# A two-layer hybrid decoder trunk: seven block products in place of eight for most chunk pairs, the residual stream in DRAM, tables and factors by ACT's DMA queue

## The chip, the cores and the metric

The kernel runs on one core of one Trainium2 chip. The metric is the device time of one execution in microseconds (us), median of three runs. TensorE (PE) has one of two clock levels granted to it, 1.2 and 2.4 GHz; the profile gives the granted share of full speed. The other engines are VectorE (DVE), ScalarE (ACT), GpSimd (POOL) and SyncE (SP), which issues DMAs.

## The reference, cut to what matters

256 tokens of width 2048 go through two layers. Each layer has a mixer sub-layer and an FFN sub-layer, all in f32.

```python
for l in range(2):
    h = rms_norm(x, g_mix_pre)                       # (256, 2048)
    proj = h @ w_in                                  # 2048 -> 512 pool | 1024 conv GLU | 4x1024 q k v gate | 3x2048 branch gates
    y_pool = pool_mixer(u_pool) @ w_pool_proj        # 512 -> 2048, window tables
    y_conv = conv_module(u_conv) @ w_conv_proj       # GLU, 31 causal taps, LayerNorm, swish; 512 -> 2048
    y_ret = retention(q, k, v, g_ret) @ w_ret_proj   # 8 heads, decay tables; 1024 -> 2048
    merged = sigmoid(gate0)*y_pool + sigmoid(gate1)*y_conv + sigmoid(gate2)*y_ret
    x = x + rms_norm(merged @ w_out, g_mix_post)     # 2048 -> 2048
    h = rms_norm(x, g_ffn_pre)
    a, b = split(h @ w_ffn_in)                       # 2048 -> 2 x 5632
    x = x + rms_norm((silu(a) * b) @ w_ffn_out, g_ffn_post)   # 5632 -> 2048
```

## The kernel before

**Products.** Tokens lie in two halves h = 0 and 1 of 128. A weight matrix is worked off in chunks of 512 columns; a chunk has one step for each 128 rows k of the weight. At a step each half multiplies its transposed activations (128x128, stationary) by the weight block (128x512, moving). Both are split into a rounded part `hi` and the rest `lo` in f32r, and one step of one half is three matmuls in `product`: hi by hi (L747), lo by hi (L748), hi by lo (L749). `multiply(h)` does one step of one half; half 1 runs `LAG` = 8 steps behind half 0. A step of both halves is called an item here.

**Weights.** `fetch` brings two steps of weights (512 KB) into one of 6 `raw` tiles by SP's DMA queue (L692); `load` makes `whi` on ACT (L725) and `wlo` on DVE (L726) for both steps, which is called a block here. There are 7 buffers of each, and `load_ahead` keeps 7 blocks ahead of half 1.

**Seven products (Strassen-Winograd).** For a pair of neighbouring chunks, two token halves, and one quad of four k, there are 2x2 times 2x2 blocks, which is eight block products of two steps each. `mixed_product` does seven (`b11`, `b21`, `t1`, `b22`, `t2`, `t3`, `t4`), each of two steps of three matmuls. It costs sums of weight blocks on DVE (L705, L712, L729, L730), three further casts to hi and lo, sums of results (L785, L790, L792, L797 on DVE, one ACT copy L770 into a `dt` tile), and one addition more per result (L578, L588). The sums of token blocks (`token_sums`, tile pair `S`) are made once for each input. Before the change this is done for k 12 to 15 of 10 of the 11 FFN-in pairs of each layer (the set `fast`); the first pair after a sub-layer's start is `paired` instead, that is, its two chunks take turns step by step.

**Order.** `chunks` lists the whole program. A layer is: pool, v, q, k, retention gate, conv gate and conv value chunks; then for each branch and column chunk a gate chunk and a projection (4 or 8 steps); 4 chunks of `w_out`; then FFN in four parts of 3, 3, 3 and 2 pairs of FFN-in, each followed by 4 FFN-out chunks over that part's hidden quads, accumulated in `og` tiles.

**Side work.** `pool_job`, `conv_job`, `ret_job` are generators; after each item of half 1 `run_jobs` gives them `BUDGET` = 0.35 of credit, in list order, at most two heavy ones at a time; a `WAIT` pauses a job for 8 ticks (a tick is one `multiply`). The conv job is 124 yields of 0.35 for its taps (L342) and 4.0 for its rest; the retention jobs of a layer cost 10.4 together. `finish` runs a job to its end at once when a chunk needs it. Transposes and splits of results are put off by `defer` (7 ticks for the hidden quads, 14 for merged quads and rotated q and k).

**Tiles.** A pool of 20 `slot` tiles of 4 KB per partition holds transposed activations (8 per input), branch results, q, k, v, hidden quads, `og`. Tag `dt` has two buffers: window and decay tables, and the two result sums of a mixed pair. The gain rows `gp` have two buffers. The residual `x0`, `x1` stays in SBUF. All DMAs go by SP's queue: weights L692, tables L378, L402, L415, pool weights L372, gain rows L548.

Of the kernel before, what the change touches and what calls it, by code (L numbers as in the profile page):

```python
# [18 lines left out]
P = 128  # L19
# [18 lines left out]
LAG = 8  # L38
WBLOCKS = 7
SLOTS = 20  # L40
# [10 lines left out]
N_WARM = 12  # L51

# [23 lines left out]
def trunk(ctx: ExitStack, tc: tile.TileContext, x, x_cols, positions, g_mix_post, g_ffn_post, w_in, pool_w,  # L76
# [38 lines left out]
    xs = []  # L115
    for h in range(2):
        xs.append(cpool.tile([P, 4, NB], F32, name=f"x{h}"))
# [25 lines left out]
    def square_sum(src, acc):  # L143
        j = t2("junk", 1)
        act.activation(j, src, ACT.Square, accum_out=acc)
# [14 lines left out]

    def pre_norm_quad(h, c, gain, mixed):
        tp, g = transpose4(xs[h][:, c, :]), gain[:, 4 * c:4 * c + 4]
        if not (mixed and c == 3):
            st["xT", h].append(split(tp, g))
            return
        if h == 0:
            st["u"] = slot([P, 2, 4, P])
        u = st["u"][:, h]
        dve.tensor_tensor(u, tp, g.unsqueeze(2).to_broadcast([P, 4, P]), op=ALU.mult)
        st["xT", h].append(split(u))  # L170
        if h == 1:
            defer(6, token_sums)

    def token_sums():

        u = st["u"]
# [3 lines left out]
        dve.tensor_tensor(s[:, 1], s[:, 0], a11, op=ALU.subtract)  # L180
        dve.tensor_tensor(s[:, 2], a11, a21, op=ALU.subtract)
        dve.tensor_tensor(s[:, 3], a12, s[:, 1], op=ALU.subtract)
        hi, lo = slot([P, 4, 2, P], F32R), slot([P, 4, 2, P], F32R)
        act.copy(hi, s)
        dve.tensor_tensor(lo, s, hi.bitcast(F32), op=ALU.subtract)
        st["S"] = (hi, lo)
# [6 lines left out]
    def sum_squares(h):  # L193
        ssq = small("ssq_n", 4)
        for c in range(4):
            square_sum(xs[h][:, c, :], ssq[:, c:c + 1])
        pre_norm_rstd(h, ssq)

    def load_x(h, c):
        nc.sync.dma_start(xs[h][:, c, :], x[0, h * P:(h + 1) * P, c * NB:(c + 1) * NB])  # L200
# [19 lines left out]
    def post_norm(h, gain, mixed=False):  # L220
# [3 lines left out]
        def residual(c):  # L224
            xc = xs[h][:, c, :]
# [14 lines left out]
        defer(N_FIRST + N_STEP * 4, sum_squares, h)  # L240

# [153 lines left out]
    def ret_job(l, h, qd):  # L395
# [4 lines left out]
        if h == 0:  # L400
            dt = t2("dt", 2, (P, 4, P))
            nc.sync.dma_start(dt, decays[qd])  # L402
# [110 lines left out]
    def ev_swish(l, qd):  # L513
        def f(h, ps):
# [5 lines left out]
            add_job(("ret", h), ret_job(l, h, qd))  # L520
        return f

    def ev_gate(h, ps):
        s = t2("sg", 3)
# [437 lines left out]
```

## Time and profile before

| | |
|---|---|
| median of 3 runs | 2876.71 us (2876.64 to 2877.05) |
| the profiled execution, its own time | 2875.82 us |
| its span, first to last instruction | 2874.1 us |
| mean granted TensorE clock | 0.999 |
| PE busy | 2855.9 us (99%) |
| DVE busy | 1947.7 us (68%) |
| ACT busy | 1356.4 us (47%) |
| DMA | 555.07 MB, 193 GB/s |

Busy time is the union of an engine's instructions. Matmuls overlap one another in the records, so their spacing is read from start to start. PEld is TensorE's weight load. SPq is SP's DMA issue queue.

### The profile page before, as it was taken

How to read it: one execution, taken by the hardware profiler on the slowest of the kernel's cores; microseconds unless marked ns; L12 is line 12 of the kernel's file. 1: busy time of each engine (PE TensorE's matmuls, PEld its weight loads, DVE VectorE, ACT ScalarE, POOL GpSimd, SP SyncE). 2: the span in 40 equal slices, each digit the busy share in tenths (PEclk: the TensorE clock that was granted, in tenths of full speed). 3: DMA queues.
4: the chain of work that ended last, by engine and by line, in shares of the span. 5: the costliest groups of instructions: out<-in, count | busy, mean ns of one | idle time of the engine just before them, and what ended most of it. 6: DMA issues, size and time to landing. Idle time of an engine off the chain costs nothing.

```text
span 2874.1 us, 34293 instructions
## 1 busy us (share of the span) xinstructions
PE 2855.9 (99%) x12932; PEld 2362.9 (82%) x12932; DVE 1947.7 (68%) x2253; ACT 1356.4 (47%) x1547; POOL 83.1 (3%) x102
## 2 busy tenths in 40 slices
PE   9999999999999999999999999999999999999998
PEld 7788888888888888888888888888888888888887
DVE  6766965555775776857765569555567757668586
ACT  5444445444644544544554444444455454445353
POOL 0000000000000000000000000001000000000000
PEclk9999999999999999999999999999999999999999
DMA  8655565556565656555655555655565555666554
GB/s 298 193 183 176 186 199 189 191 189 203 174 204 174 215 196 201 176 203 175 229 188 185 189 171 188 199 189 186 191 204 190 190 185 189 211 194 200 187 183 153
DMA packets 289862, 555.07 MB, mean 193 GB/s; under 512 B 17824, under 2 KB 21152, under 8 KB 289696
## 3 DMA queue, kind: packets, MB, share of 16 engines
q1 hardware_dynamic: 289696, 552.89, 58.5%
q8 instruction: 101, 1.65, 0.2%
q14 instruction: 65, 0.53, 0.1%
HBM read 550.72 MB, written 2.10 MB: 192 GB/s over the span
## 4 chain that ended last, share of the span: by engine, by line
PE 98%; DVE 1%; DMA 0%; POOL 0%; ACT 0%; issue 0%; SPq 0%; DVEq 0%; POOLq 0%; ACTq 0%
PE mm L748 32%; PE mm L749 32%; PE mm L747 32%; PE tp L140 2%; DVE x L226 0%; PE sc L429 0%; PE tp L421 0%; PE sc L385 0%; DVE wlo L726 0%; DVE ta L131 0%; DMA dt<-in_bands 0%; DMA par<-in_params 0%; POOL rpost_a L210 0%; PE sc L411 0%; PE tp L406 0%
## 5 line engine op out<-in xcount | busy, mean ns | idle before, releaser
L726 DVE TENSOR_TENSOR wlo<-raw,whi 128x1024 fp32r<-128x1024 f32 (+1 forms) x1085 | 1336.9, 1240 | 738.0 <-ACT whi L725 725.6
L725 ACT CAST whi<-raw 128x1024 fp32r<-128x1024 f32 (+1 forms) x1085 | 1135.4, 1052 | 1283.5 <-PE mm L748 1148.2
L747 PE MATMUL mm<-whi,slot 128*128 128x512 f32 x4056 | 1589.9, 392 | 1.9 <-ACT whi L725 1.7
L748 PE MATMUL mm<-whi,slot 128*128 128x512 f32 x4056 | 1581.1, 390 | 0.2
L749 PE MATMUL mm<-wlo,slot 128*128 128x512 f32 x4056 | 1580.9, 390 | 0.0
L749 PEld LDWEIGHTS mm<-wlo,slot 128*128 128x128 f32 x4056 | 761.8, 188 | 159.4 <-DVE wlo L726 0.7
L747 PEld LDWEIGHTS mm<-whi,slot 128*128 128x128 f32 x4056 | 762.0, 188 | 156.7 <-ACT whi L725 2.4
L748 PEld LDWEIGHTS mm<-whi,slot 128*128 128x128 f32 x4056 | 762.4, 188 | 156.1 <-DVE slot L134 2.1
L342 DVE SCALAR_TENSOR_TENSOR slot<-slot,par,slot 128x229 f32<-128x229 f32 (+23 forms) x240 | 101.9, 479 | 0.3
L134 DVE TENSOR_TENSOR slot<-tp,slot 128x512 fp32r<-128x512 f32 x60 | 41.2, 687 | 50.3 <-ACT slot L133 50.3
L133 ACT CAST slot<-tp 128x512 fp32r<-128x512 f32 x60 | 35.2, 586 | 83.3 <-PE tp L140 83.3
L538 POOL TENSOR_TENSOR slot<-slot,tb 128x512 f32<-128x512 f32 x32 | 43.3, 1352 | 639.5 <-DVE tb L537 639.5
L578 DVE TENSOR_TENSOR ta<-dt,mm 128x512 f32<-128x512 f32 x40 | 27.4, 684 | 29.9 <-PE mm L749 29.9
L218 POOL TENSOR_SCALAR ms_o<-ssq_t 128x1 f32<-128x1 f32 x8 | 3.2, 395 | 1509.0 <-DVE ssq_t L216 1509.0
L525 ACT ACTIVATE sg<-mm,rstd 128x512 f32<-128x512 f32 x48 | 33.0, 688 | 24.4 <-PE mm L749 24.2
L597 DVE TENSOR_TENSOR slot<-slot,mm 128x512 f32<-128x512 f32 x48 | 32.8, 684 | 13.0 <-PE mm L749 13.0
L140 PEld LDWEIGHTS tp<-ident,ta 128*128 128x128 f32 x272 | 34.0, 141 | 8.4
L140 PE MATMUL tp<-ident,ta 128*128 128x128 f32 x272 | 40.6, 271 | 0.0
L569 ACT ACTIVATE sg<-ta,rstd 128x512 f32<-128x512 f32 x40 | 29.0, 725 | 10.5 <-DVE ta L588 10.5
L580 DVE SCALAR_TENSOR_TENSOR ta<-ta,rstd,sg 128x512 f32<-128x512 f32 x40 | 30.0, 749 | 1.0
L133 ACT CAST slot<-ta 128x512 fp32r<-128x512 f32 x36 | 22.4, 621 | 16.4 <-DVE ta L131 16.2
L537 DVE TENSOR_TENSOR tb<-mm,sg 128x512 f32<-128x512 f32 x32 | 22.1, 690 | 9.4 <-PE mm L749 8.1
(131 smaller groups left out, 732.5 us busy)
## 6 DMA issues: line engine op xcount, KB each, us to landing
raw<-in_w_in SPq DMA_DIRECT2D x367, 512.0 KB, 3.5
raw<-in_w_ffn_in SPq DMA_DIRECT2D x352, 512.0 KB, 4.4
raw<-in_w_ffn_out SPq DMA_DIRECT2D x176, 512.0 KB, 3.7
raw<-in_w_out SPq DMA_DIRECT2D x64, 512.0 KB, 3.6
raw<-in_w_ret_proj SPq DMA_DIRECT2D x32, 512.0 KB, 3.6
raw<-in_w_pool_proj SPq DMA_DIRECT2D x16, 512.0 KB, 3.6
raw<-in_w_conv_proj SPq DMA_DIRECT2D x16, 512.0 KB, 3.8
dt<-in_decays SPq DMA_DIRECT2D x12, 256.0 KB, 3.8
```

Of the source, the lines that this page charges most:

```text
L133: act.copy(t[:, 0], src)
L134: dve.tensor_tensor(t[:, 1], src, t[:, 0].bitcast(F32), op=ALU.subtract)
L140: pe.transpose(tp[:, j, :], src[:, j * P:(j + 1) * P], ident)
L342: dve.scalar_tensor_tensor(acc[:, ct, s:], hT[:, ct, :SEQ - s], w[:, TAPS - 1 - s:TAPS - s], acc[:, ct, s:], op0=ALU.mult, op1=ALU.add)
L525: act.activation(s, ps, ACT.Sigmoid, scale=st["rstd", h])
L538: gp.tensor_tensor(m, m, t, op=ALU.add)
L597: dve.tensor_tensor(o, o, ps, op=ALU.add)
L725: act.copy(hi[:, kk:kk + step], raw[:, kk:kk + step])
L726: dve.tensor_tensor(lo[:, kk:kk + step], raw[:, kk:kk + step], hi[:, kk:kk + step].bitcast(F32), op=ALU.subtract)
L747: pe.matmul(ps, a[0], w[0], start=first, stop=False)
L748: pe.matmul(ps, a[1], w[0], start=False, stop=False)
L749: pe.matmul(ps, a[0], w[1], start=False, stop=stop)
```

## The change

Seven products in place of eight are used for more pairs: in each layer 5 pairs of gate chunks (the chunk order is changed so that gates 0 and 1 of a column chunk stand together, and gates 2 in twos), chunks 0 and 1 of `w_out`, 10 FFN-in pairs as before, and 5 pairs of FFN-out, where FFN now has three parts of 4, 4 and 3 pairs. For `w_out` and FFN-out the mixed quad is the first, k 0 to 3. `token_sums` becomes a light job and is run for six inputs a layer. The conv chunks come right after the pool chunk. The residual no longer stays in SBUF: it is stored to DRAM by SP's queue after each sub-layer but the last (`store_x`) and fetched by ACT's queue into slot tiles near the end of the next (`fetch_x`). There are 24 slots. Window and decay tables, pool weights and gain rows are loaded by ACT's queue.

```diff
-SLOTS = 20
+SLOTS = 24
...
-    xs = []
-    for h in range(2):
-        xs.append(cpool.tile([P, 4, NB], F32, name=f"x{h}"))
+    dram = ctx.enter_context(tc.tile_pool(name="stream", bufs=1, space=bass.MemoryType.DRAM))
+    xd = [[x[0, h * P:(h + 1) * P, :] for h in range(2)]]
+    for n in range(2 * DEPTH - 1):
+        xd.append([dram.tile([P, D], F32, name=f"x{n}_{h}") for h in range(2)])
...
+    def fetch_x(n, h):
+
+        st["x", h] = []
+        for c2 in range(2):
+            t = slot([P, 2, NB])
+            nc.scalar.dma_start(t, xd[n][h][:, columns(c2)].rearrange("p (c n) -> p c n", n=NB))
+            st["x", h].append(t)
+
+    def store_x(n, h, tiles):
+        for c2 in range(2):
+            nc.sync.dma_start(xd[n][h][:, columns(c2)].rearrange("p (c n) -> p c n", n=NB), tiles[c2])
...
+        st["xT", h].append(split(transpose4(x_block(h, c)), gain[:, 4 * c:4 * c + 4]))
+        if mixed and c == 3 and h == 1:
+            add_job(("sum", 0), token_sums("xT", 3), True)
+
+    def token_sums(lhs, c):
+
+        ts = [st[lhs, h][c] for h in range(2)]
+        u = slot([P, 2, 4, P])
+        for h in range(2):
+            dve.tensor_tensor(u[:, h], ts[h][:, 0].bitcast(F32), ts[h][:, 1].bitcast(F32), op=ALU.add)
+            yield 0.7
...
+        yield 0.9
...
-        st["S"] = (hi, lo)
+        st["S", lhs] = (hi, lo)
+        yield 1.2
...
         defer(N_FIRST + N_STEP * 4, sum_squares, h)
+        defer(N_STORE, store_x, n + 1, h, st["x", h])
...
-            nc.sync.dma_start(pw, pool_w[l].rearrange("g c d -> c g d"))
+            nc.scalar.dma_start(pw, pool_w[l].rearrange("g c d -> c g d"))
...
-            nc.sync.dma_start(b, bands[n])
+            nc.scalar.dma_start(b, bands[n])
...
-                nc.sync.dma_start(dt, decays[2 + qd * 2 + pr])
+                nc.scalar.dma_start(dt, decays[2 + qd * 2 + pr])
...
+            if qd == 1 and h == 1:
+                add_job(("sum", 0), token_sums("xT", 3), True)
...
+        def f(h, ps, t=None):
+            s = t2("sg", 4)
+            if t is not None:
+                dve.tensor_tensor(s, t, ps, op=ALU.add)
+                ps = s
+            act.activation(s, ps, ACT.Sigmoid, scale=st["rstd", h])
+            st["sg", h, b, c] = s
...
-            if b == 1:
+            if b == 2:
...
+                def put():
+                    st["mT", h].append(split(transpose4(m)))
+                    if h == 1 and c == 0:
+                        add_job(("sum", 0), token_sums("mT", 0), True)
+
+                defer(2 * D_T, put)
...
-            nc.sync.dma_start(g, src[c * NB:(c + 1) * NB].partition_broadcast(P))
+            nc.scalar.dma_start(g, src[c * NB:(c + 1) * NB].partition_broadcast(P))
...
+            if t is not None:
+                u = t2("ta", 3)
+                dve.tensor_tensor(u, t, ps, op=ALU.add)
+                ps = u
             post_collect(h, c, ps, bc)
+            if c == 1:
+                fetch_x(2 * l, h)
             if c == 3:
-                post_norm(h, par[l][:, C_GFFN:C_GFFN + 16], True)
+                post_norm(2 * l, h, par[l][:, C_GFFN:C_GFFN + 16], True)
...
+                hid.append(split(transpose4(u)))
+                if first and h == 1:
+                    add_job(("sum", 0), token_sums("hid", 0), True)
...
-            if part == 0:
+        def f(h, ps, t=None):
+            if part == 0 and t is None:
                 act.copy(og_tile(c, h), ps)
-                return
-            o = st["og", h, c]
-            dve.tensor_tensor(o, o, ps, op=ALU.add)
+            elif part == 0:
+                dve.tensor_tensor(og_tile(c, h), t, ps, op=ALU.add)
+            else:
+                o = st["og", h, c]
+                if t is not None:
+                    dve.tensor_tensor(o, o, t, op=ALU.add)
+                dve.tensor_tensor(o, o, ps, op=ALU.add)
             if not last:
                 return
             bc = gain_tile(c, h, g_ffn_post[l])
             post_collect(h, c, o, bc)
+            if c == 1:
+                fetch_x(2 * l + 1, h)
             if c == 3:
-                post_norm(h, par[l + 1][:, C_GPRE:C_GPRE + 16] if l + 1 < DEPTH else None)
+                post_norm(2 * l + 1, h, par[l + 1][:, C_GPRE:C_GPRE + 16] if l + 1 < DEPTH else None)
...
+        add(wi, 0, 16, Q_CG, "xT", ev_conv_g)
+        add(wi, 0, 16, Q_CA, "xT", ev_conv_a(l))
         for qd in range(2):
             add(wi, 0, 16, Q_V + qd * NB, "xT", ev_v(qd))
-        for qd in range(2):
             add(wi, 0, 16, Q_Q + qd * NB, "xT", ev_rot("qT", qd))
-        for qd in range(2):
             add(wi, 0, 16, Q_K + qd * NB, "xT", ev_rot("kT", qd))
-        for qd in range(2):
             add(wi, 0, 16, Q_R + qd * NB, "xT", ev_swish(l, qd))
-        add(wi, 0, 16, Q_CG, "xT", ev_conv_g)
...
-        for b, c in [(b, c) for c in range(4) for b in (0, 2)] + [(1, c) for c in range(4)]:
-            add(wi, 0, 16, Q_GATE + b * D + c * NB, "xT", ev_gate)
-            w, name = ((w_pool_proj, "pool"), (w_conv_proj, "conv"), (w_ret_proj, "ret"))[b]
-            add(w[l], 0, 8 if b == 2 else 4, c * NB, ("brT", b), ev_y(b, c), (name,))
         for c in range(4):
-            add(w_out[l], 0, 16, c * NB, "mT", ev_out(l, c))
+            if c:
+                mix(3)
+            for b in range(2):
+                gate(b, c, ("sum",) if c else ())
+            for b in range(2):
+                project(b, c)
+        for c2 in range(2):
+            mix(3)
+            for c in range(2):
+                gate(2, 2 * c2 + c)
+            for c in range(2):
+                project(2, 2 * c2 + c)
+        for c in range(4):
+            if c == 0:
+                mix(0)
+            add(w_out[l], 0, 16, c * NB, "mT", ev_out(l, c), ("sum",))
-        parts = ((0, 3), (3, 6), (6, 9), (9, 11))
+        parts = ((0, 4), (4, 8), (8, 11))
         for p, (b0, b1) in enumerate(parts):
+            last = p == len(parts) - 1
             for j in range(b0, b1):
-                add(w_ffn_in[l], 0, 16, j * NB, "xT", ev_a)
+                if j:
+                    mix(3)
+                add(w_ffn_in[l], 0, 16, j * NB, "xT", ev_a, ("sum",) if j else ())
                 add(w_ffn_in[l], 0, 16, HIDDEN + j * NB, "xT", ev_b(j == b0))
             for c in range(4):
-                add(w_ffn_out[l], b0 * 4, (b1 - b0) * 4, c * NB, "hid", ev_ffn(l, c, p, p == len(parts) - 1))
+                if c == 0 or c == 2 and not last:
+                    mix(0)
+                add(w_ffn_out[l], b0 * 4, (b1 - b0) * 4, c * NB, "hid", ev_ffn(l, c, p, last), ("sum",))
...
-        if n in fast:
-            for k in (0, 2, 4, 6, 8):
+        ks = list(range(0, chunks[n][2], LOAD))
+        if n in mixed:
+            q = 4 * mixed[n]
+            ks = [k for k in ks if k // 4 != mixed[n]]
+
+            head = max(LAG // LOAD, len(ks) - 1)
+            for k in ks[:head]:
                 plan("", n, k)
-            plan("b11", n, 12)
-            plan("t1", n, 12)
-            plan("", n, 10)
-            plan("b21", n, 14)
+            plan("b11", n, q)
+            plan("t1", n, q)
+            for k in ks[head:]:
+                plan("", n, k)
+            plan("b21", n, q + 2)
+            plan("b22", n, q + 2)
+            for k, kind, kq in zip(ks, ("t2", "t3", "t4"), (q, q, q + 2)):
                 plan("", n + 1, k)
-            n += 2
+                plan(kind, n, kq)
+            for k in ks[3:]:
+                plan("", n + 1, k)
+            side = (n, n + 1)
...
         if kind == "b11":
-            x = bank(x_part(0))
+            x = bank(a_part(0))
             if last:
-                st["sum", 1] = t2("dt", 2)
-                act.copy(st["sum", 1], x)
+                assert items[done[1]][1] >= n
+                st["sum", 1, n] = t2("dt", 2)
+                act.copy(st["sum", 1, n], x)
...
-                ev_a_sum(0, st["sum", 1], y)
+                outs[0](0, y, st["sum", 1, n])
...
         elif kind == "t2":
             x = bank(s_part(1))
             if last:
-                s = st["sum", 1]
+                s = st["sum", 1, n]
                 dve.tensor_tensor(s, s, x, op=ALU.add)
-                st["sum", 0] = t2("dt", 2)
-                dve.tensor_tensor(st["sum", 0], s, banks["t1", n], op=ALU.add)
+                st["sum", 0, n] = t2("dt", 2)
+                dve.tensor_tensor(st["sum", 0, n], s, banks["t1", n], op=ALU.add)
         elif kind == "t3":
             x = bank(s_part(2))
             if last:
-                s = st["sum", 1]
+                s = st["sum", 1, n]
                 dve.tensor_tensor(s, s, x, op=ALU.add)
+        elif kind == "t4":
+            y = product((1, n), "mm1", a_part(1), w, last)
+            if last:
+                assert items[done[1]][1:] > (n, final[n])
+                s = st["sum", 1, n]
+                outs[0](1, y, s)
+                dve.tensor_tensor(s, s, banks["t1", n], op=ALU.add)
...
-            if k == 0:
+            if k == (4 if mixed.get(n, mixed.get(n - 1)) == 0 else 0):
```

## Rows read from the trace of the kernel before

**Rows 1.** The page: busy times, the granted clock, the last-ended chain.

```profile
PE 2855.9 (99%) x12932; PEld 2362.9 (82%) x12932; DVE 1947.7 (68%) x2253; ACT 1356.4 (47%) x1547; POOL 83.1 (3%) x102
...
PEclk9999999999999999999999999999999999999999
...
PE 98%; DVE 1%; DMA 0%; POOL 0%; ACT 0%; issue 0%; SPq 0%; DVEq 0%; POOLq 0%; ACTq 0%
```

**Rows 2.** Waits of PE, three of five: us in total, times, longest.

```profile
PE sc L385 <- DMA dt<-in_bands: 3.0, 1, 3.0
PE mm L747 <- ACT whi L725: 1.7, 1, 1.7
PE tp L140 <- DVE x L226: 1.6, 4, 0.6
...
```

**Rows 3.** Three stretches (conv; FFN; a layer's end): busy by engine, count.

```profile
300.00:360.00 60.00, 60.00 (x266) 49.67 (x266) 60.00 (x109) 25.74 (x27) 3.57 (x2) 1.00 0.56 185
960.00:1020.00 60.00, 60.00 (x272) 49.68 (x272) 49.67 (x50) 31.77 (x34) 0.00 (x0) 1.00 0.50 164
1380.00:1440.00 60.00, 58.48 (x263) 47.23 (x262) 42.86 (x51) 30.07 (x41) 3.31 (x4) 1.00 0.65 209
```

**Rows 4.** Timeline of PE: start, duration; the first and the 49th matmul of a run.

```profile
863.23 0.39 PE L747 MATMUL mm<-whi,slot 128*128 128x512 f32 x1
...
874.11 0.39 PE L747 MATMUL mm<-whi,slot 128*128 128x512 f32 x1
```

**Rows 5.** Groups of instructions by line: busy us, mean ns, idle before, releaser.

```profile
L747 PE MATMUL mm<-whi,slot 128*128 128x512 f32 x4056 | 1589.9, 392 | 1.9 <-ACT whi L725 1.7 <-ACT slot L133 0.2
...
L726 DVE TENSOR_TENSOR wlo<-raw,whi 128x1024 fp32r<-128x1024 f32 (+1 forms) x1085 | 1336.9, 1240 | 738.0 <-ACT whi L725 725.6 <-PE tp L406 3.0 <-PE sc L411 3.0
L725 ACT CAST whi<-raw 128x1024 fp32r<-128x1024 f32 (+1 forms) x1085 | 1135.4, 1052 | 1283.5 <-PE mm L748 1148.2 <-DVE raw L705 46.1 <-issue 36.3
...
L578 DVE TENSOR_TENSOR ta<-dt,mm 128x512 f32<-128x512 f32 x40 | 27.4, 684 | 29.9 <-PE mm L749 29.9
...
L705 DVE TENSOR_TENSOR raw<-raw,raw 128x1024 f32<-128x1024 f32 x20 | 24.5, 1224 | 0.7
...
L790 DVE TENSOR_TENSOR dt<-dt,mm 128x512 f32<-128x512 f32 x20 | 13.7, 687 | 5.1 <-PE mm L749 5.1
...
L770 ACT COPY dt<-mm 128x512 f32<-128x512 f32 x20 | 11.6, 578 | 0.0
...
L185 DVE TENSOR_TENSOR slot<-slot,slot 128x1024 fp32r<-128x1024 f32 x2 | 2.5, 1225 | 0.0
...
L179 DVE TENSOR_TENSOR slot<-slot 128x256 f32<-128x256 f32 x2 | 0.8, 416 | 0.0
```

**Rows 6.** Waits of SP's DMA queue: us in total, times, longest.

```profile
SPq L692 <- DVE slot L342: 161.6, 58, 4.0
...
SPq L548 <- DVE slot L213: 20.8, 11, 10.5
...
SPq L402 <- PE sc L385: 2.8, 2, 2.0
```

**Rows 7.** The chain that ended last, layer 0: start, duration, what.

```profile
73.79 4.84 DMA dt<-in_bands
```

**Rows 8.** Timeline of SP at the start: start, duration, instruction.

```profile
0.72 0.39 SPq L378 DMA_DIRECT2D dt<-in_bands  x1
1.16 0.42 SPq L832 DMA_DIRECT2D slot<-in_x_cols  x1
```

**Rows 9.** Two lines' DMA issues: duration min/median/max ns, first and last start.

```profile
L372 SPq DMA_DIRECT2D slot<-in_pool_w x2: 468/468/469, 54.4 to 1475.2; - x2
L548 SPq DMA_DIRECT2D gp<-in_g_mix_post x8: 340/341/462, 72.8 to 2109.7; - x8
```

**Rows 10.** The page: the DMA queue of the kernel's own transfers.

```profile
q1 hardware_dynamic: 289696, 552.89, 58.5%
```

More of the change, by code (lines that the diff above doesn't have):

```diff
@@ L159, in tick, with columns, x_block @@
             fn(*args)
-    def pre_norm_quad(h, c, gain, mixed):
-        tp, g = transpose4(xs[h][:, c, :]), gain[:, 4 * c:4 * c + 4]
-        if not (mixed and c == 3):
-            st["xT", h].append(split(tp, g))
-            return
[L166 to L176, printed above, removed]
+    def columns(c2):
+        return slice(c2 * 2 * NB, (c2 + 1) * 2 * NB)
+    def fetch_x(n, h):
[7 more added lines that the diff above has]
+            nc.sync.dma_start(xd[n][h][:, columns(c2)].rearrange("p (c n) -> p c n", n=NB), tiles[c2])
+    def x_block(h, c):
+        return st["x", h][c // 2][:, c % 2, :]
+    def pre_norm_quad(h, c, gain, mixed):
+        st["xT", h].append(split(transpose4(x_block(h, c)), gain[:, 4 * c:4 * c + 4]))
[7 more added lines that the diff above has]
+            yield 0.7
         a11, a12, a21, a22 = (u[:, h, 2 * i:2 * i + 2] for h in range(2) for i in range(2))
@@ L218, in post_collect, with post_norm @@
             gp.tensor_scalar(st["ms_o", h], tot, 1.0 / D, NORM_EPS, op0=ALU.mult, op1=ALU.add)
-    def post_norm(h, gain, mixed=False):
+    def post_norm(n, h, gain, mixed=False):
         r = st["rpost", h]
@@ L574, in f @@
             if first:
                 st["hid", h] = []
[L576 to L589 removed]
+            u = t2("ta", 3)
@@ L608, in trunk, with mix, gate, project @@
     ends = []
+    mixed = {}
     def add(w, r0, kt, c0, lhs, evac, needs=()):
         chunks.append((w, r0, kt, c0, lhs, evac, needs))
+    def mix(quad):
+        mixed[len(chunks)] = quad
     for l in range(DEPTH):
         wi = w_in[l]
+        def gate(b, c, needs=()):
+            add(wi, 0, 16, Q_GATE + b * D + c * NB, "xT", ev_gate(b, c), needs)
+        def project(b, c):
+            w, name = ((w_pool_proj, "pool"), (w_conv_proj, "conv"), (w_ret_proj, "ret"))[b]
+            add(w[l], 0, 8 if b == 2 else 4, c * NB, ("brT", b), ev_y(b, c), (name,))
@@ L640, in trunk @@
+                add(w_ffn_out[l], b0 * 4, (b1 - b0) * 4, c * NB, "hid", ev_ffn(l, c, p, last), ("sum",))
         ends.append(len(chunks))
     paired = {0} | {e for e in ends[:-1]}
-    fast = {n for n, ch in enumerate(chunks) if ch[5] is ev_a and n not in paired}
     items = []
     count = {}
+    final = {}
     def plan(kind, n, k):
@@ L778, in mixed_product @@
             product((0, n + 1), "mm0", s_part(3), w, False)
-        elif kind == "t4":
-            y = product((1, n), "mm1", x_part(1), w, last)
-            if last:
-                assert items[done[1]][1:] > (n, 11)
-                s = st["sum", 1]
-                ev_a_sum(1, s, y)
-                dve.tensor_tensor(s, s, banks["t1", n], op=ALU.add)
         elif kind == "t2":
```

103 lines of the change are left out of this document (48 added, 55 removed).

## Prediction

> **What bounds the kernel now.** I read the page first, then PE's waits, then stretches of the span, the matmuls' spacing and the groups by line, and last the queues.
>
> The page: PE is busy 2855.9 us of 2874.1, and the chain that ended last lies on PE for 98% of the span; TensorE is granted the upper of its two levels, 2.4 GHz, throughout [rows 1]. PE waits for almost nothing: the longest of its waits are 3.0 us for a window table, once, and 1.7 and 1.6 us [rows 2]. In a stretch in which DVE is busy 60.00 of 60 us (the conv job), and in an FFN stretch full of seven-product pairs with DVE at 49.67, PE loses nothing; only a sub-layer's end shows 1.5 us lost [rows 3]. What protects PE is the lead of the weights: ACT waits 1148.2 us for PE to give a `whi` buffer back, so the seven blocks are nearly always full [rows 5].
>
> So time goes with the number of matmuls. One lasts 392 ns in the list [rows 5], but they overlap: 48 of them start between 863.23 and 874.11, 0.2267 us each [rows 4]. That spacing is the price. A block of two steps is 12 matmuls, 2.72 us; the seven blocks ahead are 19 us, and if ACT's casts stop, PE runs dry after about six blocks, 16.3 us.
>
> The Trainium skill (TensorE: Matmul & The Clock Gate, Back-to-back issue gap) gives about 131 ns a matmul for a sustained stream of 512 columns and about 216 ns for isolated ones. This trace shows 226.7, so the measurement decides; by 131 the saving below would be 17.3 us, by 216 it would be 28.5.
>
> **The change part by part.**
>
> *Products.* A layer has 5 mixed gate pairs, 1 of `w_out`, 10 of FFN-in and 5 of FFN-out: 21, 42 in all against 20. Each of the 22 new ones leaves out one block product of 2 steps x 3 matmuls. 22 x 6 = 132 matmuls x 0.2267 = **-29.9 us**, all on PE's path. Each of the three lines has 44 fewer, 4012 for 4056. Three FFN parts for four change no matmul and no transpose.
>
> *DVE, off the path.* A new pair costs three more `wlo` of 1.240, four weight sums of 1.224, four result sums of 0.687 and four additions of 0.684 [rows 5]: 3.72 + 4.90 + 2.75 + 2.74 = 14.1 us, 22 times 310. Token sums: 12 instead of 2, each 1.225 + 4 x 0.416 and two additions of about 0.68 [rows 5], some 4.3 us, +45 with the old form taken off. One FFN part less saves 16 additions a run, -11. DVE: 1947.7 + 344 = 2292, 80% of the new span. Pair by pair, against 186 matmuls = 42.2 us of PE: a gate pair 19 x 1.24 + 4.90 + 2.75 + 2.74 = 34 us (81%); an FFN-out pair of 16 steps with accumulation 37 us (87%). FFN-in pairs stand at the same level now and PE loses nothing beside them [rows 3]. The one pair over 100% is that of the last part, 12 steps: 15 x 1.24 + 4.90 + 2.75 + 12 x 0.684 = 34.5 us against 138 matmuls, 31.3 us. Its 3.2 us come out of the lead of 19 us, and the two plain chunks behind it (some 20 us of DVE in 32.6) give it back. Cost 0; without that cover 2 x 3.2.
>
> *ACT, off the path.* 22 x (3 x 1.052 + 0.578) = 82 us, 10 token casts, and 52 DMA issues (18 tables, 2 pool weights, 16 gain rows, 16 fetches) of 0.34 to 0.47 [rows 8, 9], about 21 us. 1356 becomes some 1470, 52%. Cost 0.
>
> *The loads moved to ACT's queue.* On SP such a load stands in front of weight fetches; gain rows made SP wait 20.8 us in 11 waits, the longest 10.5, and decay tables 2.8 for PE [rows 6]. On ACT they stand in front of `whi` casts and result copies, and for those DVE and PE wait. A stop of 10.5 is under the 16.3 that PE can bear, so I take 0; what a longer one does is a rival. At the start SP issues a table for 0.39 us before the first `x_cols` load [rows 8]; that goes, between -0.4 and 0, I take -0.4. The table that PE waited for in layer 0 landed 4.84 us after its issue [rows 7], and it still needs a `dt` buffer that half 0's product gives back: between -3.0 and +3.0, taken as 0.
>
> *The residual.* Stores of 3 x 2.1 MB, fetches of 4 x 2.1: 14.7 MB on 552.9, where the DMA engines are 58.5% busy [rows 10]. A half's fetch goes out at chunk 1's end and is read after chunk 3, two chunks later: 32 items of 1.36 = 43.5 us, in the last FFN part 24 items, 32.6. A 256 KB load took 4.84 us [rows 7]; four times that is 19.4 for the half's 1 MB. Hidden. The store is put off 28 ticks, the last residual addition 9, so SP does not stand before it. The fetch takes slot tiles. Would it be issued far ahead and hold them? Gain rows for the layer's end are issued at 72.8 us, hundreds of us early, but the pool weights of layer 1, also a slot tile and free of any input, wait until 1475.2 [rows 9]: slot tiles keep their order. FFN fills 8 (input) + 2 + 2 (sums) + 4 (`og`) + 8 (hidden) = 24 of 24 slots; before, 8 + 2 + 4 + 6 = 20 of 20. No new wait, 0.
>
> *Later reads made tighter.* `w_out` begins with k 4, so merged quad 3, transposed 14 ticks (7 items) after the last projection, is read at the 9th item instead of the 13th: about 9 matmuls, 2 us, for a cast and a subtraction. The last FFN part had that distance before, and PE's waits for such a cast are 0.2 us in the whole run [rows 5]. Between 0 and 1.6 us a layer; I take 0.
>
> *Retention beside the first mixed gate pair.* This has no row. The pool, conv gate and conv value chunks are 48 items, and 7 ticks later, near item 51, the conv job starts and eats one step's credit an item for 124 items, to about 175. Its rest (4.0), retention (10.4) and the token sums (4.4) are 18.8 credits / 0.35 = 54 items, to about 229. The first mixed gate pair starts at item 13 x 16 + 2 x 4 = 216. So the last retention steps share the two `dt` buffers and the four small PSUM banks with the pair's sums. Bounds: 0 if all is shifted behind the pair; if the pair's sums wait for a table to be loaded (4.84) and used after a pause of 8 ticks (5.4), 10 us a layer. Near the conv stretch, where a full DVE cost PE nothing [rows 3], I take 1 us a layer, **+2**.
>
> **The sum.** From the profiled execution's own 2875.8: -29.9 - 0.4 + 2 = 2847.5. The median of the runs is 0.9 above that execution: **2848.4 us**.
>
> **The rivals.**
>
> *A: the first gate pairs cost their upper bound.* Retention's tables and the pair's sums get in each other's way. For it: both tiles share tag `dt`, and nothing in the old FFN had that. Against it: the pair's other matmuls need none of these. Up to 9 us more a layer, 18 in all: 2855 to 2866.
>
> *B, the other side: a held table load stops ACT.* In the same place a decay table's load waits at the head of ACT's queue for a `dt` buffer held by a pair's result sum. The first is taken after 66 of the pair's 186 matmuls and kept to its end, 120 x 0.2267 = 27.2 us; PE bears 16.3, so a full hold costs 10.9. It decides from the fourth on: two in each layer, 43.6, bring 2892. For it: SP's queue did stand at such loads, the longest 10.5 us [rows 6]. Against it: that is the longest, and tables wanted by a layer are few. The Trainium skill (Perfetto Trace Analysis, DMA Instruction - HWDGE) says that the issuing sequencer itself sits out a DMA's semaphore wait, which is what those SP rows show; by it the casts behind a held load wait as well.
>
> *C: DVE's lead is spent.* The 12-step pair's 3.2 us fall on PE because the pairs before it (86 to 87%) leave no lead, just before a layer's end where PE already loses 1.5 [rows 3]: 2 x 3.2, 2855.
>
> That the change doesn't do what it says can be left out: the count of pairs follows from the lists in the diff.
>
> **How the numbers follow.** Forecast case, 2842 to 2853: 0.70. C, 2853 to 2857: 0.10. A, up to 2866: 0.14. B: 0.06. The measurement can tell about 0.2%, 5.8 us, from no change, so faster means under 2871. The forecast, C and most of A are faster, 0.90; the rest of A with its waits added up, and B with two or three holds, 0.04 the same; B with four, 0.06 with what I have not seen. The range goes from 2842 (the window table's wait gone, no cost at the gates) to 2862 (A by two thirds); outside lie some 0.15.
>
> **What would show it.** Right: 4012 matmuls a line at an unchanged 0.2267 spacing, PE busy near 2827, DVE near 2290, ACT under 1500, PE's waits still near ten us in all, the span some 28 shorter. Wrong: PE waiting for `whi` behind an ACT that waits for a `dt` or `gp` tile (B); PE waiting on small-bank sums or retention in the stretch some 300 us into a layer (A); PE waiting for `wlo` in the last 60 us of a layer (C); `x` tiles landing after the residual addition wants them. A shortfall with no PE wait would mean a wrong spacing.

## The result, and the profile after

The changed kernel takes **2858.61 us** (median of 4 runs, 2854.81 to 2859.58) beside 2876.68 for the kernel before on the same chip: a ratio of 0.9935, 95% interval 0.9918 to 0.9953. It is 18 us faster; 28 had been forecast. The profiled execution took 2859.58 us, with a span of 2857.8. One execution of a kernel below (the residual fetched later) took 3544.62 us at a granted clock of 0.752, and its ratio leaves that one out.

The page of the changed kernel, its busy times, two DMA queues (q10 is ACT's) and the chain that ended last, to be read beside [rows 1, 10]:

```profile
PE 2830.9 (99%) x12800; PEld 2338.9 (82%) x12800; DVE 2232.8 (78%) x2641; ACT 1427.6 (50%) x1630; POOL 108.7 (4%) x102
...
q1 hardware_dynamic: 285472, 549.74, 57.9%
q10 hardware_dynamic: 8256, 17.83, 1.9%
...
PE 95%; DVE 2%; DMA 1%; ACT 0%; issue 0%; POOL 0%; SPq 0%; DVEq 0%; POOLq 0%; ACTq 0%
```

PE is busy 25 us less, and the chain is on PE for 95% of the span, no longer 98%: DVE and DMA have come into it. Its groups by line, the matmuls and the weight work (beside [rows 5]):

```profile
L826 PE MATMUL mm<-whi,slot 128*128 128x512 f32 x4012 | 1572.5, 392 | 4.1 <-ACT whi L804 4.0
...
L805 DVE TENSOR_TENSOR wlo<-raw,whi 128x1024 fp32r<-128x1024 f32 (+1 forms) x1151 | 1399.0, 1233 | 446.7 <-ACT whi L804 435.6 <-PE sc L408 3.4 <-DMA slot<-in_x 2.0
L804 ACT CAST whi<-raw 128x1024 fp32r<-128x1024 f32 (+1 forms) x1151 | 1195.2, 1052 | 1207.7 <-PE mm L827 847.2 <-DVE raw L784 111.1 <-DVE raw L809 69.7
```

The 4012 matmuls a line are those of the forecast. The reserve has become thinner: ACT waits 847 us for PE to give a `whi` buffer back, and 1148 before. PE's waits (beside [rows 2]):

```profile
PE mm L828 <- DVE wlo L805: 6.5, 6, 2.0
PE mm L826 <- ACT whi L804: 4.0, 1, 4.0
PE sc L402 <- DMA dt<-in_bands: 2.6, 1, 2.6
...
PE sc L446 <- DVE ta L441: 0.4, 1, 0.4
PE tp L142 <- DVE tb L461: 0.3, 1, 0.3
```

All rows of this view add up to 17.3 us, and to 8.0 before. The first row is new: six times PE stood for a `wlo` from DVE. Where that happens shows in stretches; an FFN stretch and a layer's end in the changed kernel, beside [rows 3] (length; PE, PEld, DVE, ACT, POOL busy and counts; granted clock, DMA share, GB/s):

```profile
960.00:1020.00 60.00, 60.00 (x269) 49.69 (x268) 44.39 (x45) 28.25 (x30) 0.00 (x0) 1.00 0.67 220
...
1380.00:1440.00 60.00, 56.69 (x248) 45.74 (x248) 45.68 (x56) 28.06 (x38) 2.05 (x4) 0.97 0.80 268
```

The middle of FFN loses nothing, as before. In the last 60 us of layer 0 PE is busy 56.69 us in place of 58.48, its clock is lowered for a part of it (0.97), and the DMA engines are 80% busy in place of 65%.

Waits alone miss what a lower clock costs, so the table below is worked out from PE's timeline. From each distance between one start and the next, what a matmul of its shape usually takes is taken off (0.2267 us for 512 columns), and what is left is added up by stretch. It is time lost, in us. What is "usual" for the small matmuls shifts the sums of a stretch by some tenths, and those of the start and the whole span by a few us; the differences between two kernels hardly move:

| place | before | changed |
|---|---|---|
| first 60 us | 3.1 | 7.1 |
| the window table, 60 to 100 us | 3.2 | 3.1 |
| first mixed gate pairs, layer 0 / layer 1 | 0.1 / -0.1 | 2.3 / 0.2 |
| the `w_out` pair's beginning, 573 and 1992 us | 0.1 / 0.0 | 1.3 / 1.3 |
| the last FFN part's 12-step pair, 1398 and 2817 us | -0.3 / -0.3 | 4.0 / 1.7 |
| layer end, 1415 to 1465 us | 3.0 | 2.6 |
| whole span | 10.8 | 24.3 |

Without the losses the span was 2863.3 and is 2833.5: 29.8 us for the products. That follows from the count of matmuls and their usual distance, which is 0.2267 us in both kernels, so it confirms these two and nothing else. The losses took 13.5 of it back. Each place is looked at by itself, and the experiments go by places.

### The profile page after: what moved, and what is told of

The parts are those of the page before. It is cut to its first block, busy times and chain, and to the rows that moved or that the text cites. A ratio compares the mean times of both kernels' runs of the same rounds, so it can differ in the third digit from the quotient of the medians.

```text
span 2857.8 us, 34682 instructions
## 1 busy us (share of the span) xinstructions
PE 2830.9 (99%) x12800; PEld 2338.9 (82%) x12800; DVE 2232.8 (78%) x2641; ACT 1427.6 (50%) x1630; POOL 108.7 (4%) x102
## 4 chain that ended last, share of the span: by engine, by line
PE 95%; DVE 2%; DMA 1%; ACT 0%; issue 0%; POOL 0%; SPq 0%; DVEq 0%; POOLq 0%; ACTq 0%
PE mm L828 31%; PE mm L827 31%; PE mm L826 31%; PE tp L142 2%; DVE wlo L805 1%; DMA raw<-in_w_ffn_out 1%; ACT whi L804 0%; PE sc L446 0%; DMA raw<-in_w_in 0%; PE tp L438 0%; PE sc L402 0%; DMA dt<-in_bands 0%; DVE slot L136 0%; DVE slot L242 0%; PE tp L423 0%
## 5 line engine op out<-in xcount | busy, mean ns | idle before, releaser
L804 ACT CAST whi<-raw 128x1024 fp32r<-128x1024 f32 (+1 forms) x1151 | 1195.2, 1052 | 1207.7 <-PE mm L827 847.2
L805 DVE TENSOR_TENSOR wlo<-raw,whi 128x1024 fp32r<-128x1024 f32 (+1 forms) x1151 | 1399.0, 1233 | 446.7 <-ACT whi L804 435.6
L826 PE MATMUL mm<-whi,slot 128*128 128x512 f32 x4012 | 1572.5, 392 | 4.1 <-ACT whi L804 4.0
L827 PE MATMUL mm<-whi,slot 128*128 128x512 f32 x4012 | 1564.6, 390 | 0.6 <-DVE slot L136 0.6
L828 PEld LDWEIGHTS mm<-wlo,slot 128*128 128x128 f32 x4012 | 754.0, 188 | 166.1 <-DVE wlo L805 9.6
L826 PEld LDWEIGHTS mm<-whi,slot 128*128 128x128 f32 x4012 | 754.3, 188 | 158.4 <-ACT whi L804 5.3
L827 PEld LDWEIGHTS mm<-whi,slot 128*128 128x128 f32 x4012 | 754.6, 188 | 155.8 <-DVE slot L136 2.7
L359 DVE SCALAR_TENSOR_TENSOR slot<-slot,par,slot 128x229 f32<-128x229 f32 (+25 forms) x240 | 98.1, 461 | 0.5
L136 DVE TENSOR_TENSOR slot<-tp,slot 128x512 fp32r<-128x512 f32 x60 | 40.8, 685 | 47.4 <-ACT slot L135 47.4
L563 POOL TENSOR_TENSOR slot<-slot,tb 128x512 f32<-128x512 f32 x32 | 56.9, 1782 | 542.0 <-DVE tb L562 503.2
L784 DVE TENSOR_TENSOR raw<-raw,raw 128x1024 f32<-128x1024 f32 x42 | 51.4, 1223 | 1.2
L808 DVE TENSOR_TENSOR raw<-raw,raw 128x1024 f32<-128x1024 f32 x42 | 52.1, 1241 | 0.1
L809 DVE TENSOR_TENSOR raw<-raw,raw 128x1024 f32<-128x1024 f32 x42 | 51.3, 1221 | 0.9
L791 DVE TENSOR_TENSOR raw<-raw,raw 128x1024 f32<-128x1024 f32 x42 | 51.1, 1218 | 0.1
L147 ACT ACTIVATE tb<-slot 128x512 f32<-128x512 f32 x48 | 30.0, 626 | 20.6 <-DVE slot L642 14.5
```

What stands on the lines that cost most here:

```text
L359: dve.scalar_tensor_tensor(acc[:, ct, s:], hT[:, ct, :SEQ - s], w[:, TAPS - 1 - s:TAPS - s], acc[:, ct, s:], op0=ALU.mult, op1=ALU.add)
L563: gp.tensor_tensor(m, m, t, op=ALU.add)
L784: dve.tensor_tensor(kept["b11"], kept["b12"], kept["b11"], op=ALU.subtract)
L804: act.copy(hi[:, kk:kk + step], raw[:, kk:kk + step])
L805: dve.tensor_tensor(lo[:, kk:kk + step], raw[:, kk:kk + step], hi[:, kk:kk + step].bitcast(F32), op=ALU.subtract)
L808: dve.tensor_tensor(kept["b12"], raw, kept["b12"], op=ALU.subtract)
```

## The experiments

Every run was compared with the kernel before on the same chip; the ratio is to that. Four executions of one kernel spread by 1 to 5 us, so a difference of 1 or 2 us between two medians shows nothing by itself; what a place costs is read from the traces. "Lost" is by the table's reckoning, in one profiled execution of each kernel.

**The start.** ACT's timeline at the start of the changed kernel:

```profile
0.72 0.89 ACTq L395 DMA_DIRECT2D dt<-in_bands  x2
1.63 0.96 ACTq L579 DMA_DIRECT2D gp<-in_g_mix_post  x2
...
9.54 0.62 ACT L804 CAST whi<-raw 128x512 fp32r<-128x512 f32 x1 [2.48 <-DMA raw<-in_w_in]
```

The gain rows (`gp`), wanted near the end of the first mixer sub-layer, are loaded 1.63 us into the span; before, the first went out at 72.8 [rows 9]. On ACT's queue only two tables stand ahead of them. The first cast waits 2.48 us for raw weights.

*Gain rows on SP's queue again:*

```diff
-            nc.scalar.dma_start(g, src[...].partition_broadcast(P))
+            nc.sync.dma_start(g, src[...].partition_broadcast(P))
```

> The changed kernel with the gain rows loaded by SP's queue again. Theory S (crowding at the start): the changed kernel's first weight cast waits 3.98 us for PE's view because 768 KB of tables and gain rows now go out in the first 3 us beside the first weights; without the two gain rows (512 KB) PE's first real matmul comes near 8 us instead of 10.2 and the start's loss falls from 7.0 us to about 4, the total by some 3 us (about 2855.5). Rival (the order on SP alone, with the second layer's parameters in front, or chance): first matmul still near 10, total unchanged within 1 us. Elsewhere SP stands at gain rows as before the change; both expect nothing from that.

Measured 2852.02 us (ratio 0.9917, 0.9902 to 0.9932), so 6.6 less, twice what was expected. ACT's timeline at the start of this kernel:

```profile
0.71 0.89 ACTq L395 DMA_DIRECT2D dt<-in_bands  x2
...
6.92 1.14 ACT L804 CAST whi<-raw 128x512 fp32r<-128x512 f32 x2
```

The cast comes 2.6 us earlier and waits for no DMA. SP's queue shows one reason: the same three weight loads in the changed kernel, and then in this one:

```profile
2.13 2.68 SPq L771 DMA_DIRECT2D raw<-in_w_in  x3
```

```profile
2.13 1.38 SPq L771 DMA_DIRECT2D raw<-in_w_in  x3
```

SP takes 1.3 us longer to issue them when the gain rows go out beside them on ACT's queue; it takes 2.68 to 2.74 in eight profiles with the rows there and 1.38 in five with them on SP. 3.2 us are lost in the first 60 us in place of 7.1, and 1.5 in place of 3.1 at the window table. The start varies from kernel to kernel: it lost 2.9 to 5.2 us in the four profiles of a changed kernel with gain rows on SP and 6.0 to 7.1 in the seven with them on ACT. By the means, 4.0 and 6.3, the gain rows' place in the queue is worth some 2.4 us at the start. This kernel's start is one of the better ones (in the kernel of three changes below, rows also on SP, the first cast waits 1.60 us for raw weights), and the rest of the 6.6, at the window table and in the 12-step pair (4.5 lost in place of 5.7), is not shown to come from the gain rows.

*The kernel before with the tables, pool weights and gain rows on ACT's queue:*

> The kernel before with one part of the change alone: tables, pool weights and gain rows by ACT's queue. Theory S: the start loses what the changed kernel's start loses, first real matmul near 10 us instead of 8, +3 to +4 us, about 2880; nothing elsewhere. Rival (the start's loss comes from other parts of the change): within 1 us of before. Rival B of the prediction (a held load stops ACT) would show PE waiting for whi late in a layer, +5 or more.

Measured 2876.26 us (0.9999, 0.9990 to 1.0009). The start loses 5.6 in place of 3.1 and the window table 1.8 in place of 3.2. The time did not move, though the start's loss did occur: 2.5 more there, 1.4 given back at the table, and the 1.1 between them is too little for the medians to show. No load held ACT there.

**The 12-step pair.** The chain that ended last in the changed kernel, just before its stop at 1398 us:

```profile
1382.12 2.36 DVE wlo L805 x2
1384.48 0.02 issue
1384.50 12.15 DMA raw<-in_w_ffn_out
...
1396.73 0.50 ACT whi L804
...
1399.12 1.15 DVE wlo L805
```

The chain runs from a late `wlo` on DVE, which frees a `raw` tile, through a weight load that takes 12.15 us to the cast and the `wlo` that PE waits for. Two things are in it, DVE's work and a slow load (512 KB; the median of all loads of `w_ffn_out` is 4.9 us). ACT's timeline in that stretch shows what is loaded beside it:

```profile
1383.93 0.33 ACTq L171 DMA_DIRECT2D slot<-x  x1
1390.13 1.05 ACT L804 CAST whi<-raw 128x1024 fp32r<-128x1024 f32 x1 [5.17 <-DMA raw<-in_w_ffn_out]
1390.14 0.35 ACTq L171 DMA_DIRECT2D slot<-x  x1
```

L171 is `fetch_x`, the residual.

*The last part's pair with all eight products:* `if c in (0, 2) and not last: mix(0)`.

> The changed kernel with the FFN-out pair of the last FFN part computed plainly (two pairs fewer, 12 matmuls more, +2.7 us of PE). Theory D (that pair asks DVE for 34.5 us in 31.3 of PE): the losses at 1380 to 1410 us (3.9) and at 2800 (1.9) go away, net about -3 us, 2855.5. Theory F (the residual's fetch, 2 MB, fills the DMA engines there): the losses stay, net +2.7, 2861.

Measured 2855.38 us (0.9928, 0.9913 to 0.9943). Both losses are gone (0.0), though 12 matmuls, 2.7 us, came back. By places the pair as changed costs more (5.7) than it saves.

*Four additions of the residual sum `og` in this pair on GpSimd in place of DVE* (and in the two FFN-out pairs of the second part):

```diff
                 if t is not None:
-                    dve.tensor_tensor(o, o, t, op=ALU.add)
+                    gp.tensor_tensor(o, o, t, op=ALU.add)
```

> The changed kernel with the four additions of the residual in the last FFN-out pair on GpSimd in place of VectorE. Theory: VectorE's lead is spent in this pair of 12 steps (34.5 us of work beside 31.3 of TensorE); without four additions of 0.68 it has 2.7 us less to do there, and the losses at 1380 to 1410 us and at 2816 us (5.8 in sum) fall to under 2, all mixed pairs kept: about 2854.5. Rival: the late fetch of raw weights beside fetch_x sets the loss; then it stays at 5 to 6 and the time at 2858.6. If GpSimd's slower additions delay the stores, the end of a layer grows by 1 to 2 us.

Measured 2853.77 us (0.9923, 0.9908 to 0.9937): 4.8 less, all pairs kept. The two losses fall to 0.6 and 0.8. The edit also takes 16 additions off DVE in the second part's pairs, where nothing was lost. The row of these additions in a later kernel that keeps this edit (count; duration min/median/max in ns; first and last start):

```profile
L641 POOL TENSOR_TENSOR slot<-slot,dt x24: 1290/2207/2218, 1157.4 to 2807.2; 128x512 f32<-128x512 f32 x24
```

2.2 us each in place of 0.684 on DVE is slow, but PE hardly pays for it. The Trainium skill (GPSIMD Engine Reference, 3.1 Elementwise) has an f32 addition of 2048 elements 1.96 times as long on GpSimd as on VectorE; here, with 512 elements and by GpSimd's spans in the profile, which are rough, it is 3.2 times.

*The residual fetched one chunk later (`if c == 2` in `ev_ffn`), in two runs:*

> The changed kernel with the residual's fetch at the end of FFN issued one chunk later (after chunk 2 instead of chunk 1), so that it does not meet the mixed pair's weights. Theory F: the losses at 1380 to 1410 and 2800 shrink from 5.8 us together to under 2, total near 2854.5. Theory D: weights are late because DVE gives raw tiles back late, so the losses stay at 4 to 6 us, total unchanged within 1.5 us.

> The kernel of the late fetch once more, for its profile: fetch_x of the last FFN part at chunk 2 in place of chunk 1. If VectorE's lead alone sets the loss in the 12-step pair, 3.9 and 1.9 us stand near 1398 and 2817 us as in the changed kernel, and casts still wait for raw weights there. If the 2 MB of the residual delay the raw weights, the two losses fall by half or more, and, the time being unchanged, a new loss of 2 to 4 us stands behind it, where the residual is wanted at the layer's end.

Measured 2857.85 (0.9937, 0.9920 to 0.9954) and 2858.25 us (0.9940, 0.9918 to 0.9963); rows are from the second. The losses stand (2.0 and 2.0). But the edit did not do what it was meant to. The issues of L171 from 1300 to 1500 us, in the changed kernel and then in this one (count; duration min/median/max; first and last start):

```profile
L171 ACTq DMA_DIRECT2D slot<-x x4: 326/334/354, 1373.3 to 1390.1; - x4
```

```profile
L171 ACTq DMA_DIRECT2D slot<-x x4: 327/338/356, 1373.7 to 1390.1; - x4
```

The transfers went out at the same times. Where the call stands in the code does not set them, so these runs tell nothing of the transfers. They are in effect a second profile of the changed kernel, and show that the loss in layer 0 can be 2.0 as well as 4.0.

*The residual at the ends of FFN not fetched at all:* GpSimd fills the tiles with zeros, which leaves the residual out of these two additions.

```diff
-            nc.scalar.dma_start(t, xd[n][h][...])
+            if n % 2:
+                gp.memset(t, 0.0)
+            else:
+                nc.scalar.dma_start(t, xd[n][h][...])
```

> The changed kernel without the residual's fetch at the ends of FFN: GpSimd fills its four slot tiles with zeros, so the residual is left out of these two additions; 2.1 MB less are moved beside each 12-step pair. If the transfers delay the raw weights there, casts stop waiting for them, the losses near 1398 us (3.9) and 2817 us (1.9) fall to under 2 in sum, and the time falls by about 4, to 2854.5. If VectorE's lead alone is spent, the losses stand at 5 to 6 and the time stays at 2858.6.

Measured 2852.32 us (0.9918, 0.9901 to 0.9934): 6.3 less, and both losses are gone (0.1). The stretch from 1370 to 1410 us, columns as above, in the changed kernel:

```profile
1370.00:1410.00 40.00, 38.02 (x163) 30.85 (x161) 33.42 (x38) 20.23 (x27) 0.00 (x0) 0.96 0.78 271
```

Without the fetch:

```profile
1370.00:1410.00 40.00, 40.00 (x180) 33.00 (x179) 34.66 (x40) 21.92 (x30) 0.19 (x1) 1.00 0.75 250
```

With the additions on GpSimd, and then with the pair plain:

```profile
1370.00:1410.00 40.00, 39.72 (x178) 32.59 (x177) 33.88 (x37) 22.01 (x30) 7.79 (x5) 1.00 0.85 299
```

```profile
1370.00:1410.00 40.00, 40.00 (x180) 33.14 (x179) 24.91 (x27) 19.21 (x26) 0.19 (x1) 1.00 0.78 257
```

Without the fetch DVE does more work in the stretch than in the changed kernel (34.66 us to 33.42, all the additions of the pair among it), and PE loses nothing. So DVE's work alone does not spend the lead. The time to landing of the 11 weight loads that go out from 1375 to 1396 us, in the changed kernel, without the fetch, and with the additions on GpSimd:

```profile
DMA to landing us min/median/max: 4.5/8.9/12.3
```

```profile
DMA to landing us min/median/max: 4.2/5.4/6.3
```

```profile
DMA to landing us min/median/max: 4.8/8.8/11.6
```

Beside the residual a weight load takes 8.9 us by the median, without it 5.4. ACT's waits for raw weights of `w_ffn_out` in the whole run (us, times, longest), in the changed kernel and without the fetch:

```profile
ACT whi L804 <- DMA raw<-in_w_ffn_out: 13.5, 9, 5.2
```

```profile
ACT whi L807 <- DMA raw<-in_w_ffn_out: 1.3, 2, 0.7
```

With the additions on GpSimd the loads are as slow as in the changed kernel and the waits for raw weights remain (16.6 us in 15), yet PE hardly loses. The loss needs both: the pair's full work on DVE, and 2.1 MB of residual in the same 20 us, which makes the weight loads slow. Taking either away ends it. That DVE's part in it is the late freeing of `raw` tiles is what the chain above shows; no run changes that alone.

**The merged token sums.** DVE's timeline before PE's stop at 573 us in the changed kernel:

```profile
564.62 1.23 DVE L805 TENSOR_TENSOR wlo<-raw,whi 128x1024 fp32r<-128x1024 f32 x1 [1.45 <-ACT whi L804]
...
566.96 1.28 DVE L191 TENSOR_TENSOR slot<-slot 128x512 f32<-128x512 f32 x2
568.16 0.68 DVE L562 TENSOR_TENSOR tb<-mm,sg 128x512 f32<-128x512 f32 x1
568.76 1.21 DVE L784 TENSOR_TENSOR raw<-raw,raw 128x1024 f32<-128x1024 f32 x1
569.90 1.51 DVE L195 TENSOR_TENSOR slot<-slot 128x256 f32<-128x256 f32 x1
...
572.00 1.21 DVE L808 TENSOR_TENSOR raw<-raw,raw 128x1024 f32<-128x1024 f32 x1
573.14 2.35 DVE L805 TENSOR_TENSOR wlo<-raw,whi 128x1024 fp32r<-128x1024 f32 x2
```

Between two `wlo`, 7.3 us from the end of one to the start of the next, stand the transposed quad's splits, most of the sums for `w_out` (L191 to L198), a gate product and two weight sums of the pair.

*These sums' additions on GpSimd:* in `token_sums`, `gp` in place of `dve` for `mT`.

> The changed kernel with the additions of the merged token sums on GpSimd in place of VectorE. Theory: at 573 and 1992 us VectorE's merged token sums stand ahead of the next wlo, 1.2 us each; without them these two waits vanish: 2.4 less, about 2856. Rival: GpSimd finishes the sums later than VectorE did and the first product of the sums waits for them; then each place costs as much as before or 2 to 5 us more: 2858 to 2868.

Measured 2860.13 us (0.9942, 0.9925 to 0.9958): not faster. The rival holds by places: 2.1 are lost at each, not 1.3; the median's 1.5 is no more than noise. A row of ACT's waits shows why:

```profile
ACT slot L203 <- POOL slot L200: 9.8, 2, 4.9
```

ACT's cast of the sums waits 4.9 us for GpSimd each time, and the next `whi` stands behind it.

**Retention beside the gate pairs.** *`BUDGET` 0.45 in place of 0.35*, so that jobs are done sooner:

> The changed kernel with BUDGET at 0.45, so that retention work is paid out evenly through the gates. If the 2.3 us lost at 320 to 347 us into the span (layer 0 only) come from retention that is forced in late beside the mixed gate pair, that loss goes and the time falls by about 2, to 2856.5. Rival: the loss comes from VectorE's demand for the pair's own sums and weights, wherever the retention lies; then the site stays at 2 or more and the time is unchanged at 2858.6. If the budget moves too much work to other pairs, new losses of about 1 us stand there.

Measured 2854.50 us (0.9924, 0.9910 to 0.9939). PE's waits at 337 to 347 us are gone, two of them for retention's work on DVE (L441 and L461, shown above), and a new one of 1.3 us stands at 287 us:

```profile
PE tp L142 <- DVE ta L373: 1.3, 1, 1.3
```

L373 is in the conv job, not in retention. By places, 200 to 360 us, this kernel loses 1.0 less than the changed one, and so do the three combined kernels below that keep this budget, within 0.1; in layer 1 all four lose 0.3 more. So the budget is worth some 0.7 of the 4.1 that the median fell. The rest of its profile's gain lies at the window table (2.0 for 3.1) and in the 12-step pair (2.6 for 4.0), for which the budget is not shown to be the cause. That retention stands in the way at 337 to 347 us is borne out by the two waits and by their going; but the budget speeds the other jobs too, and puts a wait for one of them in the place of what it saves.

**Together.** *All four:* gain rows on SP, additions and token sums on GpSimd, `BUDGET` 0.45.

> All of it together: the gain rows on SP's queue again, the four additions of the last FFN-out pair and the merged token sums on GpSimd, BUDGET 0.45. If the places are independent, the gains add: 2858.6 less 6.6 (measured for the gain rows) less some 4, 2 and 2.4, so 2843 to 2846. Rival: relieving one place only moves VectorE's wait to the next one; then the time stays near the 2852 of the gain rows alone.

Measured 2850.78 us (0.9911, 0.9896 to 0.9926), only 1.2 below the 2852.02 of the gain rows alone, with ranges that overlap, and 5 to 8 short of the sum of the gains: the token sums on GpSimd still lose 2.1 at two places and the first 60 us lose 4.5.

*Without the token sums on GpSimd:*

> The three that helped, without the one that did not: gain rows on SP's queue, the four additions of the last FFN-out pair on GpSimd, BUDGET 0.45, and the token sums on VectorE as in the changed kernel. The version with all four stands at 2850.78; GpSimd's token sums cost 0.8 more at each of two places there (2.0 against 1.2), so 1.6 less is expected: 2849.2 (2848 to 2850). Rival: the places interact and the time stays within 0.5 of 2850.8.

Measured **2849.68 us** (0.9911, 0.9897 to 0.9924), the lowest median of the study, and 8.9 under the changed kernel. From the version with all four it is not told apart by time (1.1 less); by places the token sums lose 1.3 again in place of 2.0.

*The same with the `w_out` pair plain* (no `mix(0)` and no token sums for `mT`):

> The same three, and the first pair of output chunks with all eight products, so without its merged token sums. Theory: at 573 and 1992 us the sums and the pair's weights stand together ahead of a wlo; without them the two losses of 1.2 go, and six matmuls more in each layer cost 12 x 0.2267 = 2.7: 0.3 to 0.4 more than with the pair mixed, so this pair is worth almost nothing. Rival: the wait there comes from the gate pair that ends before it; then the losses stay and the time is 2.7 higher.

Measured 2849.95 us (0.9911, 0.9897 to 0.9924). The losses at 573 and 1992 us are gone (0.1 and 0.0), and the 12 matmuls cost 2.7. The stretch from 560 to 580 us in the changed kernel, and with the pair plain:

```profile
560.00:580.00 20.00, 19.09 (x90) 15.51 (x89) 17.06 (x20) 10.14 (x12) 2.20 (x1) 1.00 0.30 97
```

```profile
560.00:580.00 20.00, 20.00 (x92) 16.54 (x91) 19.74 (x20) 12.06 (x14) 2.21 (x1) 1.00 0.44 128
```

Seven products there are worth nothing that can be measured. DVE's busy time does not tell the two rows apart (17.06 with the loss, 19.74 without it). This run takes away the token sums and the pair's weight sums together, so which of them holds the `wlo` up is not separated.

## Why the prediction was right, and where its terms were off

The mechanism and the main term were right: 132 matmuls at 0.2267 us were to take 29.9 off, and the span without losses fell by 29.8. The sum came out at 2847.5 for the profiled execution, which took 2859.58. The time lies in the stated range, but outside the forecast case (2842 to 2853, to which 0.70 was given): it fell where only rival A was to reach, and A's losses at the gates, 2.5 in all, did not bring it there. That several terms taken as 0 added up to a time still inside the range is in part luck. Of the prediction's own signs C's came true, PE waiting for `wlo` in the last 60 us of layer 0, and PE's waits rose from 8.0 to 17.3 where near ten had been forecast. The 12.1 between sum and measurement, by the prediction's own terms:

- **The start**, "I take -0.4": measured +4.0. The one table that SP no longer issued was priced at 0.39, but a load of parameters (L263) took its place, and the first `x_cols` load went out at 1.15 us, before at 1.16. The loads that ACT's queue lets go ahead were not priced. The gain rows account for some 2.4 of the loss. The rest of the start's variation is not settled.
- **The 12-step pair**, "Cost 0; without that cover 2 x 3.2": measured 4.3 and 2.0, 6.3 in sum beside the 6.4 of rival C, and in C's place. That the sizes agree is luck: 1.7 of it is a stretch at the lower clock (last section), and the profile with the same transfers lost 2.0 and 2.0. C's reason, that earlier pairs leave no lead, does not hold by itself. The step that failed is **the residual**, "Hidden, 0". It was asked whether the residual would come in time, and it did; what it does to the weight loads beside it was not asked. Its 19.4 us for 1 MB were worked out from one load of 4.84; the weight loads of 512 KB beside it took 8.9 by the median and up to 12.3, without it 5.4. The fetch also went out while the pair was running, at 1373.3 to 1390.1, not at chunk 1's end. The Trainium skill (DMA: Bandwidth & Descriptors, Issuing engines are not separate DMA queues) says that transfers issued by different engines end up on the same 16 DMA engines and interleave; the run without the fetch agrees, with waits for raw weights at 1.3 us in place of 13.5.
- **Token sums**, costed as DVE work off the path: +2.5, at the two `w_out` pairs. An average load of 80% says nothing of one stretch in which sums, splits and the pair's own work stand between two `wlo` for 7.3 us.
- **Retention**, "+2", 1 us a layer: 2.2 in layer 0 and 0.3 in layer 1. The size was right; it is not shared evenly. Rival A's upper bound was not reached.
- **Later reads made tighter**, 0: PE waits once, 0.6 us, for a split (L136), at a layer's end; none at `w_out`.
- **The window table**, 0: measured -0.1.
- The layer end (-0.4) and all other stretches (-1.3) make up the rest: 4.4 + 6.3 + 2.5 + 0.5 - 1.8 = 11.9 of the 12.1.

Between the medians the miss is 10.2, since the changed kernel's median lies 1.0 under its profiled execution and 0.9 had been added for that of before.

Rival B did not occur: no load held ACT so that PE ran dry, and PE's one wait for a `whi` (4.0 us) is at the start. DVE was forecast at 2292 and came to 2232.8. The durations of its instructions add up to 334 us more than before, near the 344 taken; but instructions that follow each other closely overlap in the records (five `wlo` in 5.76 us, 1.15 each, where 1.24 was taken), and busy time, their union, rose by 285. ACT came to 1427.6 for 1470: 21 of the forecast were issues, which are not counted as busy, and 9 are copies into `og` that DVE now does. The reckoning of which pair is over 100% stayed useful in spite of this: it pointed at the pair with the largest loss.

## What to carry to other kernels

A load moved to an emptier queue can go out far earlier than it is wanted (here at 1.63 us in place of 72.8): at the start it can delay what the first matmul needs, and beside a crowded pair it lengthens the weight loads (here from 5.4 to 8.9 us). Price a hidden transfer by what else is loaded in the same 20 us, and a pair's work on VectorE by its own stretch and not by the engine's share of the span. Before the last such pair is made cheaper on TensorE, ask what it saves (1.36 us a pair here) beside the 1.2 to 4 us that one emptied lead costs.

## What the hardware showed unasked

A stop of PE can cost twice. PE's timeline in the changed kernel around the 12-step pair's stop:

```profile
1400.31 0.50 PE L828 MATMUL mm<-wlo,slot 128*128 128x512 f32 x1 [1.98 <-DVE wlo L805]
...
1401.35 0.40 PE L826 MATMUL mm<-whi,slot 128*128 128x512 f32 x1
1401.58 0.60 PE L827 MATMUL mm<-whi,slot 128*128 128x512 f32 x1
...
1403.25 0.63 PE L828 MATMUL mm<-wlo,slot 128*128 128x512 f32 x1
1403.68 0.63 PE L826 MATMUL mm<-whi,slot 128*128 128x512 f32 x1
```

After the wait of 1.98 us the matmuls soon start 0.43 us apart for some 3 us: the lower level, with a granted clock of 0.72 from 1400 to 1406 us. The stretch cost 1.7 us, beside 2.1 for the wait. In the kernel with `BUDGET` 0.45 a wait of 2.17 at the same place was followed by no such stretch (granted clock 1.00), and neither was one of 1.61 in the kernel with the residual's call moved. Which of the two happens did not go by the length of the wait, and its cause stays open.
